# Which split weights of the output projection are kept for the second chunk, and where a PSUM pair's x updates stand

## The chip, the cores and the metric

The kernel runs on one core of a Trainium2 chip. The metric is the device time of one execution in microseconds, lower is better; a version's time is the median of its runs. Five engines work side by side, each through its own instructions in order: TensorE (PE, with its weight loads as PEld), VectorE (DVE), ScalarE (ACT), GpSimd (POOL) and SyncE (SP), which here issues the DMA transfers. PE runs at one of two clocks, 1.2 and 2.4 GHz; the profile gives the granted clock as a share of the higher one.

## The reference

Two layers of a transformer-like trunk, for 128 prompt tokens and 512 latent tokens with the same weights, D_MODEL = 1024. Of a layer, cut to the part around the change:

```python
ga, gb, gc = jnp.split(jax.nn.sigmoid(h @ p['w_gate'] + p['b_gate']), 3, axis=-1)
merged = ga * (oa @ p['w_br_a']) + gb * (ob @ p['w_br_b']) + gc * (oc @ p['w_br_c'])
x = x + g1 * (merged @ p['w_out'])
h2 = _rmsnorm(x, p['norm2']) * (1 + sc2) + sh2
a, g = jnp.split(_dwconv3(h2 @ p['w_up'], p['conv_w'], p['conv_b']), 2, axis=-1)
x = x + g2 * ((jax.nn.silu(a) * g) @ p['w_down'])
```

`oa`, `ob` and `oc` are the outputs of a differential attention, a grouped-query attention and a pooling mixer; `h` is the modulated RMS norm of `x`; `g1`, `g2`, `sc2`, `sh2` are modulations. Everything is in float32.

## The kernel before

All 640 tokens lie side by side in the free dimension, features on the 128 partitions; a matrix of 1024 features is eight tiles of 128 (`ND` = 8). A float32 product is made of three matmuls: `split` (L94 to L96) takes an operand apart into a high part, which ACT copies in the narrower format `F32R`, and a low part, which DVE gets by subtraction; `mm3` (L111 to L114) adds high by low (L112), low by high (L113) and high by high (L114). `load_w` (L98) fetches one tile of weights into a buffer `st` (three of them go round) and splits it into `wh` and `wl`. These normally lie in a ring of five buffers, `wp`, which all weights of the program share; with `keep` they lie in another pool. Matmuls over tokens work on two chunks of 320 (`CH_B`). A `Wide` PSUM tile has two halves of 512 columns, of which 320 are used; three such tiles are used in turn for gates (`gp`), branches (`bp`), the output projection (`wo`) and the MLP (`up`).

A layer runs through these phases: attention, merge, `merged`, `out_phase`, MLP. In the merge each branch is eight tiles: a gate, a branch product, their product on DVE (L812, into the gate's tile `gt`) and, for the last branch, its sum with what the others gave, also on DVE (L813, into one of eight tiles `m32`, in the rows `m`). `merged` splits `m32` into `mh` and `ml`, the low halves of the first chunk on DVE, of the second on POOL.

`out_phase` (L842) then multiplies by w_out: for each chunk eight output tiles, two to a PSUM tile (`wo`), each of 8 x 3 = 24 matmuls. In the first chunk each w_out tile is fetched and split; tiles 0 to 6 are kept for the second chunk in the pool `wk`, and tile 7, which comes first there, is still in the ring. `wk` is opened after the merge's pool `mg` is closed, in the place that `mg` had: seven pairs of weight tiles overlap its buffers for gates, for the split branch outputs and for `m32`, so a split into them waits for the last reader of what lies there. Behind each tile DVE updates x (L862), ACT squares it (L165), and the squares are added (L168 to L171). At a chunk's end `rstd320` makes the norm factor, with two small uses of PE (`stat`, L829, and `bc`, L838 and L839), and `modulate` makes `h2h` and `h2l` (L206 to L209). The first three tiles of w_up follow, whose matmuls for the first chunk run while the second chunk is normalised.

No order is written out by hand: the program is written phase by phase, and a scheduler sets the order of the instructions on each engine from what depends on what. For PSUM the dependence is by whole tile: a matmul that writes half of a `wo` tile comes behind an x update that reads the other half, if the update stands ahead of it in the program. The engines then run in the order so found.

Of the kernel before, what the change touches and what calls it, by code (L numbers as in the profile page):

```python
# [46 lines left out]
def _segs(a, b):  # L47
    out = []
    if a < NP:
        out.append((a, min(b, NP), 0))  # L50
    if b > NP:
        out.append((max(a, NP), b, 1))
    return out
# [3 lines left out]
def trunk_kernel(ctx: ExitStack, tc: tile.TileContext, a: dict):  # L57
# [4 lines left out]
    def tp(name, bufs=1, stack=None, **kw):  # L62
        return (stack or ctx).enter_context(
            tc.tile_pool(name=name, bufs=bufs, reuse_waits="tile", **kw))
# [29 lines left out]
    def split(x, hi, lo, eng=vec):  # L94
        act.activation(hi, x, AF.Copy)  # L95
        eng.tensor_tensor(out=lo, in0=x, in1=hi.bitcast(F32), op=ALU.subtract)  # L96

    def load_w(src, cols, eng=vec, after=None, keep=None):  # L98
        st = wp.tile([P, 1024], F32, tag="st", name="st", bufs=3)
        if after is not None:  # L100
            pool.tensor_copy(st[:, 0:1], after)
        dma(st[:, :cols], src)
        hi = (keep or wp).tile([P, 1024], F32R, tag="wh", name="wh")
        lo = (keep or wp).tile([P, 1024], F32R, tag="wl", name="wl")
        split(st[:, :cols], hi[:, :cols], lo[:, :cols], eng)
        return hi, lo
# [4 lines left out]
    def mm3(out, sh, sl, mh, ml, start, stop):  # L111
        pe.matmul(out, sl, mh, start=start, stop=False)  # L112
        pe.matmul(out, sh, ml, start=False, stop=False)  # L113
        pe.matmul(out, sh, mh, start=False, stop=stop)  # L114
# [727 lines left out]
    def out_phase(l, x, rp, mh, ml, hp, wk, ps_d, first):  # L842


        A2 = scale_cols(l, V_N2, 32, "A2")
        B2 = mods[l][:, 24:32, :]
        h2h, h2l, W = [], [], {}
        for c, (a0, b0) in enumerate(CH_B):
            acc = Acc(rp, 320)
            order = (list(range(8)), [7] + list(range(7)))[c]  # L850
            for n0 in range(0, 8, 2):
                ps = ps_d.tile("wo")
                for j in range(2):
                    n = order[n0 + j]
                    if c == 0:
                        W[n] = load_w(a["w_out"][l, n], 1024, keep=wk if n < 7 else None)
                    hi, lo = W[n]
                    for k in range(ND):
                        ks = slice(k * P, (k + 1) * P)
                        mm3(ps[:, j, :320], hi[:, ks], lo[:, ks], mh[c][:, k], ml[c][:, k], k == 0, k == 7)  # L860
                    for s, e, jj in _segs(a0, b0):
                        vec.scalar_tensor_tensor(out=x[:, n, s:e], in0=ps[:, j, s - a0:e - a0],  # L862
                                                 scalar=mods[l][:, 16 + n, jj:jj + 1], in1=x[:, n, s:e],
                                                 op0=ALU.mult, op1=ALU.add)
                    acc.add(x[:, n, a0:b0], n0 + j == 7)
            h2h.append(hp.tile([P, 8, 320], F32R, tag=f"h{c}", name=f"h2h{c}"))
            h2l.append(hp.tile([P, 8, 320], F32R, tag=f"l{c}", name=f"h2l{c}"))
            modulate(rp, x, rstd320(wk, acc.acc), A2, B2, a0, b0, h2h[c], h2l[c])
        ups = ((0, 0), (1, 0), (0, 1))
        ws = []  # L870
        for c in range(2):
            for i, (part, f) in enumerate(ups):
                if c == 0:
                    ws.append(load_w(a["w_up"][l, part * F_T + f], 1024))
                    first[part, f] = ps_d.tile("up")
                hi, lo = ws[i]
                for k in range(ND):
                    ks = slice(k * P, (k + 1) * P)
                    mm3(first[part, f][:, c, :320], hi[:, ks], lo[:, ks], h2h[c][:, k], h2l[c][:, k], k == 0, k == 7)
        return h2h, h2l  # L880

    def mlp_up(l, f, h2h, h2l, mp, ps_d, first):
        vs = []
# [40 lines left out]
    rp = tp("rp", 2, xst)  # L924
    x = xp.tile([P, ND, T], F32, name="x")
    hst = ExitStack()
    hp = tp("h1p", 1, hst, side="right")
# [3 lines left out]
    ps_d = open_dense(dst)  # L931
# [76 lines left out]
    for l in range(L):  # L1008
        dst.close()
        xst.close()  # L1010
        attention_phase(l, hh, hl, w0)
        w0 = None
        xst = ExitStack()
        xp = tp("xp", 1, xst)
        rp = tp("rp", 2, xst)
        modp = tp("modp", 1, xst)
        x = xp.tile([P, ND, T], F32, name="x")
        dst = ExitStack()
        ps_d = open_dense(dst)
        with ExitStack() as ms:  # L1020
            mp = tp("mg", 1, ms)
            cs = modp.tile([P, 2, 1024], F32, tag="cs", name="cs", bufs=1)
            msteps = mod_steps(l, range(2, 6), modp, cs)
            m32 = merge_phase(l, x, cs, hh, hl, mp, ps_d, msteps)
            hst.close()
            hst = ExitStack()
            hp = tp("h2p", 1, hst, side="right")
            mh, ml = merged(m32, hp)
        first = {}
        with ExitStack() as ms:  # L1030
            h2h, h2l = out_phase(l, x, rp, mh, ml, hp, tp("wk", 7, ms), ps_d, first)
        with ExitStack() as ms:
            mp = tp("mlp", 1, ms)
            ups = {}
            if l + 1 < L:
                msteps = chain(msteps, mod_steps(l + 1, range(2), modp, cs))

            def up_to(f):
                for i in range(len(ups), f):
                    ups[i] = mlp_up(l, i, h2h, h2l, mp, ps_d, first)  # L1040
                    for _ in range(1 if i < GROUPS[0][1] + 2 else 2):
                        next(msteps, None)

            for gi, (f0, f1) in enumerate(GROUPS):
                up_to(min(F_T, f1 + 2))
                fs = [ups[f] for f in range(f0, f1)]
                nf = f1 - f0
                last = gi == len(GROUPS) - 1
                if not last:
                    for n in range(8):  # L1050
                        hi, lo = load_w(a["w_down"][l, n, :, f0 * P:f1 * P], nf * P)
                        ps = ps_d.tile("dn")
                        for c, (a0, b0) in enumerate(CH_B):
                            for i in range(nf):
                                ks = slice(i * P, (i + 1) * P)
                                mm3(ps[:, c, :320], hi[:, ks], lo[:, ks], fs[i][0][:, a0:b0], fs[i][1][:, a0:b0],
                                    i == 0, i == nf - 1)
                        for c, (a0, b0) in enumerate(CH_B):
                            down_add(l, x, n, ps[:, c], a0, b0)
                    continue  # L1060
                hst.close()
                if l + 1 < L:
                    hst = ExitStack()
                    hp = tp("h1p", 1, hst, side="right")
                    hh = hp.tile([P, ND, T], F32R, name="hh")
                    hl = hp.tile([P, ND, T], F32R, name="hl")
                    A1 = scale_cols(l + 1, V_N1, 8, "A1")
                for c, (a0, b0) in enumerate(CH_A):
                    acc = Acc(rp, b0 - a0)
                    for n0 in range(0, 8, 2):  # L1070
                        ps = ps_d.tile("dl")
                        for j in range(2):
                            n = n0 + j
                            hi, lo = load_w(a["w_down"][l, n, :, f0 * P:f1 * P], nf * P)
                            for i in range(nf):
                                ks = slice(i * P, (i + 1) * P)
                                mm3(ps[:, j, :b0 - a0], hi[:, ks], lo[:, ks], fs[i][0][:, a0:b0],
                                    fs[i][1][:, a0:b0], i == 0, i == nf - 1)
                            down_add(l, x, n, ps[:, j], a0, b0)
                            if l + 1 < L:  # L1080
                                acc.add(x[:, n, a0:b0], n == 7)
                                dma(x_dram[:, n, a0:b0], x[:, n, a0:b0])
                            else:
                                dma(a["y"][:, n, a0:b0], x[:, n, a0:b0])
                    if l + 1 < L:
                        rms1_chunk(l + 1, c, rp, x, hh, hl, ps_d, acc, A1)
# [114 lines left out]
```

## Time and profile before

| what | us |
|---|---|
| median of 3 runs | 2310.14 (2308.59 to 2310.95) |
| profiled execution, its own time | 2315.32 |
| its span, from the first to the last instruction | 2312.3 |
| PE busy in the span | 2222.7 |
| mean granted clock of PE | 0.987 |

The stage that the change touches takes, in each layer, about 80 us: from 637.7 to 717.8 us in layer 0 and from 1771 to 1852 us in layer 1, from the last `bp` matmul to the first `up` matmul of the second chunk. Of the profile the waits (who waited for whom), the timeline (each instruction with its start, its duration and the idle time ahead of it) and the windows (busy times and granted clock of a stretch) are used. A matmul's duration overlaps that of the next one; what counts for PE is the step from start to start.

### The profile page before, as it was taken

How to read it: one execution, taken by the hardware profiler on the slowest of the kernel's cores; microseconds unless marked ns; L12 is line 12 of the kernel's file. 1: busy time of each engine (PE TensorE's matmuls, PEld its weight loads, DVE VectorE, ACT ScalarE, POOL GpSimd, SP SyncE). 2: the span in 40 equal slices, each digit the busy share in tenths (PEclk: the TensorE clock that was granted, in tenths of full speed). 3: DMA queues.
4: the chain of work that ended last, by engine and by line, in shares of the span. 5: the costliest groups of instructions: out<-in, count | busy, mean ns of one | idle time of the engine just before them, and what ended most of it. 6: DMA issues, size and time to landing. Idle time of an engine off the chain costs nothing. (4 is left out here: it accounts for less than half of the span.)

```text
span 2312.3 us, 37780 instructions
## 1 busy us (share of the span) xinstructions
PE 2222.7 (96%) x14770; PEld 2165.9 (94%) x14770; DVE 1537.7 (66%) x2885; ACT 962.7 (42%) x1712; POOL 519.4 (22%) x647
## 2 busy tenths in 40 slices
PE   8998999999989999999989989999998999999999
PEld 4898989999989999999979989899998999999999
DVE  6877687569566756765587866864894476554555
ACT  5455555432244423333455546643223354242422
POOL 4652443024021000000047533320421200000000
PEclk8999999999999999999999999999999999999999
DMA  7211223366231233432242112224852132322123
GB/s 262 73 56 59 82 71 105 119 245 221 83 119 58 102 107 121 135 104 86 81 122 83 64 42 83 98 87 151 282 193 77 61 109 92 92 65 91 50 84 114
DMA packets 100469, 250.10 MB, mean 108 GB/s; under 512 B 19266, under 2 KB 32322, under 8 KB 100291
## 3 DMA queue, kind: packets, MB, share of 16 engines
q1 hardware_dynamic: 100292, 247.70, 32.8%
q8 instruction: 116, 1.90, 0.3%
q14 instruction: 61, 0.50, 0.1%
HBM read 224.72 MB, written 22.95 MB: 107 GB/s over the span
## 5 line engine op out<-in xcount | busy, mean ns | idle before, releaser
L112 PE MATMUL up<-h2h,wl 128*128 128x320 f32 x1408 | 432.7, 308 | 3.9 <-ACT h2h L208 2.5
L113 PE MATMUL up<-h2l,wh 128*128 128x320 f32 x1408 | 433.6, 308 | 0.2
L114 PE MATMUL up<-h2h,wh 128*128 128x320 f32 x1408 | 433.6, 308 | 0.0
L95 ACT ACTIVATE wh<-st 128x1024 fp32r<-128x1024 f32 (+3 forms) x320 | 297.6, 937 | 273.9 <-PE dn L114 169.6
L96 DVE TENSOR_TENSOR wl<-st,wh 128x1024 fp32r<-128x1024 f32 (+3 forms) x320 | 356.1, 1117 | 53.8 <-ACT wh L95 53.3
L112 PEld LDWEIGHTS up<-h2h,wl 128*128 128x128 f32 x1408 | 263.5, 188 | 4.6 <-ACT h2h L208 2.7
L113 PEld LDWEIGHTS up<-h2l,wh 128*128 128x128 f32 x1408 | 264.0, 188 | 0.7 <-DVE h2l L209 0.7
L114 PEld LDWEIGHTS up<-h2h,wh 128*128 128x128 f32 x1408 | 264.0, 188 | 0.0
L143 DVE SCALAR_TENSOR_TENSOR junk<-stm,cs 128x1024 bf16<-128x1024 f32 x172 | 221.7, 1289 | 63.0 <-DMA stm<-in_w_mod 60.0
L901 DVE SCALAR_TENSOR_TENSOR v<-u,vecs,v 128x127 f32<-128x127 f32 (+1 forms) x176 | 89.0, 547 | 183.2 <-ACT v L898 183.2
L112 PE MATMUL mm<-wh,hl 128*128 128x384 f32 x480 | 171.5, 357 | 12.4 <-ACT raw L361 8.5
L113 PE MATMUL dn<-al,wh 128*128 128x320 f32 x544 | 168.1, 309 | 0.0
L114 PE MATMUL dn<-ah,wh 128*128 128x320 f32 x544 | 168.1, 309 | 0.0
L112 PE MATMUL dn<-ah,wl 128*128 128x320 f32 x544 | 168.1, 309 | 0.0
L113 PE MATMUL mm<-wl,hh 128*128 128x384 f32 x480 | 165.6, 345 | 2.1 <-DVE wl L96 2.1
L114 PE MATMUL mm<-wh,hh 128*128 128x384 f32 x480 | 165.3, 344 | 0.0
L114 PE MATMUL gp<-hh,wh 128*128 128x320 f32 x480 | 148.5, 309 | 0.0
L112 PE MATMUL gp<-hh,wl 128*128 128x320 f32 x480 | 148.4, 309 | 0.0
L113 PE MATMUL gp<-hl,wh 128*128 128x320 f32 x480 | 148.2, 309 | 0.0
L112 PE MATMUL mmu<-hh,wl 128*128 128x384 f32 (+1 forms) x416 | 133.8, 322 | 3.9 <-ACT up L677 2.0
L114 PE MATMUL mmu<-hh,wh 128*128 128x384 f32 (+1 forms) x416 | 130.9, 315 | 0.0
L113 PE MATMUL mmu<-hl,wh 128*128 128x384 f32 (+1 forms) x416 | 130.1, 313 | 0.0
(232 smaller groups left out, 5434.9 us busy)
## 6 DMA issues: line engine op xcount, KB each, us to landing
stm<-in_w_mod SPq DMA_DIRECT2D x88, 512.0 KB, 4.3
st<-in_w_up SPq DMA_DIRECT2D x88, 512.0 KB, 3.6
st<-in_w_gate SPq DMA_DIRECT2D x48, 512.0 KB, 3.8
st<-in_w_unit SPq DMA_DIRECT2D x48, 384.0 KB, 3.2
st<-in_w_down SPq DMA_DIRECT2D x48, 320.0 KB, 2.9
st<-in_w_br SPq DMA_DIRECT2D x24, 512.0 KB, 3.6
st<-in_w_down SPq DMA_DIRECT2D x32, 384.0 KB, 3.2
st<-in_w_out SPq DMA_DIRECT2D x16, 512.0 KB, 4.3
```

Of the source, the lines that this page charges most:

```text
L95: act.activation(hi, x, AF.Copy)
L96: eng.tensor_tensor(out=lo, in0=x, in1=hi.bitcast(F32), op=ALU.subtract)
L112: pe.matmul(out, sl, mh, start=start, stop=False)
L113: pe.matmul(out, sh, ml, start=False, stop=False)
L114: pe.matmul(out, sh, mh, start=False, stop=stop)
L143: vec.scalar_tensor_tensor(out=junk, in0=st, scalar=1.0, in1=cs[:, j], op0=ALU.mult, op1=ALU.mult, accum_out=col)
L901: vec.scalar_tensor_tensor(out=v[:, s + 1:e], in0=u[:, s:e - 1], scalar=cw[0], in1=v[:, s + 1:e], op0=ALU.mult, op1=ALU.add)
```

## The change

`wk` holds four pairs of weight tiles instead of seven, for tiles 2 to 5. Tiles 0, 1, 6 and 7 go into the ring. The second chunk goes through the tiles in the order 6, 7, 2, 3, 4, 5, 0, 1; tiles 6 and 7 are then still in the ring, and tiles 0 and 1 are fetched and split a second time. By the addresses of the built programs, `wk` before reached over the gates' tiles, the branch operands and into `m32`; now it ends ahead of `m32`, but still lies over the others. The x updates of a PSUM pair stand in a loop of their own behind the matmuls of both tiles. The first w_up tiles have moved into a function of their own with the same code.

```diff
@@ out_phase @@
-            order = (list(range(8)), [7] + list(range(7)))[c]
+            order = (list(range(8)), (6, 7, 2, 3, 4, 5, 0, 1))[c]
             for n0 in range(0, 8, 2):
                 ps = ps_d.tile("wo")
                 for j in range(2):
                     n = order[n0 + j]
-                    if c == 0:
-                        W[n] = load_w(a["w_out"][l, n], 1024, keep=wk if n < 7 else None)
+                    if c == 0 or n < 2:
+                        W[n] = load_w(a["w_out"][l, n], 1024, keep=wk if 2 <= n < 6 else None)
                     hi, lo = W[n]
                     for k in range(ND):
                         ks = slice(k * P, (k + 1) * P)
                         mm3(ps[:, j, :320], hi[:, ks], lo[:, ks], mh[c][:, k], ml[c][:, k], k == 0, k == 7)
+                for j in range(2):
+                    n = order[n0 + j]
                     for s, e, jj in _segs(a0, b0):
                         vec.scalar_tensor_tensor(out=x[:, n, s:e], in0=ps[:, j, s - a0:e - a0],
...
+        if first is not None:
+            up_first(l, h2h, h2l, ps_d, first)
+        return h2h, h2l
+
+    def up_first(l, h2h, h2l, ps_d, first):
+
         ups = ((0, 0), (1, 0), (0, 1))
...
-            h2h, h2l = out_phase(l, x, rp, mh, ml, hp, tp("wk", 7, ms), ps_d, first)
+            h2h, h2l = out_phase(l, x, rp, mh, ml, hp, tp("wk", 4, ms), ps_d, first)
```

The scheduler's order changes in three places that matter here. Rows give the line, the instruction, what it writes and reads, and how often it stands there in a row.

DVE in layer 0, the last branch of the merge (two of its eight tiles), before:

```order
L96 TENSOR_TENSOR wl<-st,wh 128x1024
L812 TENSOR_TENSOR gt<-bp,gt 128x640
L813 TENSOR_TENSOR m_5599<-m_5599,gt 128x640
L812 TENSOR_TENSOR gt<-bp,gt 128x640
L813 TENSOR_TENSOR m_5569<-m_5569,gt 128x640
```

and after:

```order
L96 TENSOR_TENSOR wl<-st,wh 128x1024 x2
L812 TENSOR_TENSOR gt<-bp,gt 128x640
L813 TENSOR_TENSOR m_5599<-m_5599,gt 128x640
L96 TENSOR_TENSOR wl<-st,wh 128x1024
L812 TENSOR_TENSOR gt<-bp,gt 128x640
L813 TENSOR_TENSOR m_5569<-m_5569,gt 128x640
```

The two added splits are those of w_out's tiles 0 and 1; on ACT the copies that belong to them have moved likewise, between the sigmoids of the last gates.

DVE some ten instructions later, where the merge ends and the output projection begins, before:

```order
L812 TENSOR_TENSOR gt<-bp,gt 128x640
L813 TENSOR_TENSOR m_5506<-m_5506,gt 128x640
L96 TENSOR_TENSOR ml_7154<-m_5506,mh_7152 128x320
L96 TENSOR_TENSOR wl<-st,wh 128x1024 x5
L862 SCALAR_TENSOR_TENSOR x<-wo,mod_88,x 128x128
L862 SCALAR_TENSOR_TENSOR x<-wo,mod_88,x 128x192
```

and after:

```order
L812 TENSOR_TENSOR gt<-bp,gt 128x640
L813 TENSOR_TENSOR m_5506<-m_5506,gt 128x640
L96 TENSOR_TENSOR ml_7154<-m_5506,mh_7152 128x320
L96 TENSOR_TENSOR wl<-st,wh 128x1024 x3
L864 SCALAR_TENSOR_TENSOR x<-wo,mod_88,x 128x128
L864 SCALAR_TENSOR_TENSOR x<-wo,mod_88,x 128x192
L864 SCALAR_TENSOR_TENSOR x<-wo,mod_88,x 128x128
L864 SCALAR_TENSOR_TENSOR x<-wo,mod_88,x 128x192
```

Five splits stood behind the merge's last split, those of tiles 0 to 4; now there are three, of tiles 2 to 4, and the x updates of two tiles stand together.

PE in layer 0's output projection, first chunk, at the start of tile 1 (the numbers tell buffers apart; `wl_7198` and `wl_7234`, after it `wl_7228`, are tiles 0 and 1, `wl_7270` is tile 2, and `wo_7194` is the PSUM tile of tiles 0 and 1), before:

```order
L114 MATMUL wo_7266<-mh0_7152,wh_7269 128x320
L112 MATMUL wo_7337<-mh0_7152,wl_7341 128x320
L113 MATMUL wo_7337<-ml0_7154,wh_7340 128x320
L112 MATMUL wo_7194<-mh0_7152,wl_7234 128x320
L113 MATMUL wo_7194<-ml0_7154,wh_7233 128x320
```

and after:

```order
L113 MATMUL wo_7194<-ml0_7154,wh_7197 128x320
L114 MATMUL wo_7194<-mh0_7152,wh_7197 128x320
L112 MATMUL wo_7194<-mh0_7152,wl_7228 128x320
L113 MATMUL wo_7194<-ml0_7154,wh_7227 128x320
L114 MATMUL wo_7194<-mh0_7152,wh_7227 128x320
```

Before, tile 1 came behind tile 2 and the first two matmuls of tile 4; now the tiles of a pair follow each other, and the pairs stand in the order of the program. Layer 1 has the same order in all these places.

PE in layer 1's attention, ahead of a block of the input projection (`mmu`; `tr` are transposes, `sc` scores, `pv` products with values), before:

```order
L545 MATMUL sc<-qk 128x128 x8
L113 MATMUL pv<-pl,v_12949 128x128
L114 MATMUL pv<-ph,v_12949 128x128
L292 MATMUL tr<-ident,dup 128x128
L112 MATMUL mmu<-hh,wl 128x256
```

and after:

```order
L545 MATMUL sc<-qk 128x128 x8
L113 MATMUL pv<-pl,v_12961 128x128
L114 MATMUL pv<-ph,v_12961 128x128
L292 MATMUL tr<-ident,dup 128x128 x5
L112 MATMUL mmu<-hh,wl 128x256
```

Four transposes of the next group have moved ahead of the block; further places near it move with them on PE, ACT and DVE. Layer 0's attention has the order that it had.

## Rows read from the trace of the kernel before

**Rows 1.** Page: engines busy, share, instructions; a DMA group, KB each, us to land.

```profile
PE 2222.7 (96%) x14770; PEld 2165.9 (94%) x14770; DVE 1537.7 (66%) x2885; ACT 962.7 (42%) x1712; POOL 519.4 (22%) x647
...
st<-in_w_out SPq DMA_DIRECT2D x16, 512.0 KB, 4.3
```

**Rows 2.** Waits, 600 to 730 us, PE: waiter, releaser, us in all, times, longest.

```profile
PE wo L112 <- DVE wl L96: 6.1, 1, 6.1
PE up L112 <- ACT h2h L208: 1.2, 1, 1.2
PE wo L112 <- DVE x L862: 0.9, 1, 0.9
```

**Rows 3.** Timeline, PE, layer 0: start, duration, instruction, idle time before, releaser.

```profile
637.09 0.31 PE L114 MATMUL bp<-oh,wh 128*128 128x320 f32 x1
...
637.53 0.31 PE L114 MATMUL bp<-oh,wh 128*128 128x320 f32 x1
643.96 0.60 PE L112 MATMUL wo<-mh,wl 128*128 128x320 f32 x1 [6.13 <-DVE wl L96]
...
647.57 0.47 PE L113 MATMUL wo<-ml,wh 128*128 128x320 f32 x1
647.83 0.35 PE L114 MATMUL wo<-mh,wh 128*128 128x320 f32 x1
```

**Rows 4.** Windows: length, busy PE, PEld, DVE, ACT, POOL; PEclk; DMA, GB/s.

```profile
640.00:660.00 20.00, 16.04 (x97) 16.07 (x98) 12.79 (x16) 10.52 (x12) 2.73 (x3) 0.83 0.59 188
1334.00:1344.20 10.20, 8.61 (x39) 8.23 (x40) 8.03 (x17) 3.27 (x10) 0.17 (x4) 0.50 0.17 51
```

**Rows 5.** Timeline, PE, layer 1: the same place as rows 3.

```profile
1770.92 0.31 PE L114 MATMUL bp<-oh,wh 128*128 128x320 f32 x1
1777.36 0.61 PE L112 MATMUL wo<-mh,wl 128*128 128x320 f32 x1 [6.13 <-DVE wl L96]
...
1781.20 0.31 PE L114 MATMUL wo<-mh,wh 128*128 128x320 f32 x1
```

**Rows 6.** Timeline, DVE, then ACT, layer 0, from the merge's end on.

```profile
638.73 1.40 DVE L813 TENSOR_TENSOR m<-m,gt 128x640 f32<-128x640 f32 x1
640.67 0.53 DVE L96 TENSOR_TENSOR ml<-m,mh 128x320 fp32r<-128x320 f32 x1 [0.54 <-ACT mh L95]
641.97 4.12 DVE L96 TENSOR_TENSOR wl<-st,wh 128x1024 fp32r<-128x1024 f32 x3 [0.78 <-ACT wh L95]
...
654.75 1.23 DVE L96 TENSOR_TENSOR wl<-st,wh 128x1024 fp32r<-128x1024 f32 x1 [0.99 <-ACT wh L95]
640.16 0.83 ACT L95 ACTIVATE mh<-m 128x320 fp32r<-128x320 f32 x2 [2.47 <-DVE m L813]
640.90 2.93 ACT L95 ACTIVATE wh<-st 128x1024 fp32r<-128x1024 f32 x3
648.13 1.06 ACT L95 ACTIVATE wh<-st 128x1024 fp32r<-128x1024 f32 x1 [4.29 <-DMA st<-in_w_out]
```

**Rows 7.** Timeline, SP's queue, layer 0: issue and time until the group's last landing.

```profile
643.84 8.32 SPq L102 DMA_DIRECT2D st<-in_w_out  x5
```

**Rows 8.** Timeline, DVE, layer 0, in the merge's last branch.

```profile
623.86 0.82 DVE L812 TENSOR_TENSOR gt<-bp,gt 128x640 f32<-128x640 f32 x1 [8.95 <-PE bp L114]
```

**Rows 9.** Timeline, PE, the waits in the first chunk of layers 0 and 1.

```profile
668.12 0.42 PE L112 MATMUL wo<-mh,wl 128*128 128x320 f32 x1 [0.87 <-DVE x L862]
1802.12 0.41 PE L112 MATMUL wo<-mh,wl 128*128 128x320 f32 x1 [1.54 <-DVE x L862]
```

**Rows 10.** Timeline, DVE, layer 0, end of the second chunk.

```profile
708.33 0.55 DVE L862 SCALAR_TENSOR_TENSOR x<-wo,mod,x 128x320 f32<-128x320 f32 x1 [6.49 <-PE wo L114]
...
713.58 0.16 DVE L832 TENSOR_SCALAR ms<-stat 128x3 f32<-128x3 f32 x1 [3.54 <-PE stat L829]
```

**Rows 11.** Waits, 1320 to 1420 us, PE: the first and last of eight.

```profile
PE pt L495 <- DVE qk L296: 2.8, 1, 2.8
...
PE pt L467 <- DVE qk L300: 0.3, 1, 0.3
```

More of the change, by code (lines that the diff above doesn't have):

```diff
@@ L879, in out_phase @@
                     mm3(first[part, f][:, c, :320], hi[:, ks], lo[:, ks], h2h[c][:, k], h2l[c][:, k], k == 0, k == 7)
-        return h2h, h2l
     def mlp_up(l, f, h2h, h2l, mp, ps_d, first):
```

## The prediction

> **What bounds the kernel now.** The page comes first: TensorE (PE) is busy for 96% of the span, and the next engine for 66% [rows 1]. So a microsecond is to be had only where PE stands still or runs slowly, and work moved to the other engines is free as long as PE isn't made to wait for it. The question is therefore where PE waits inside the stage that the diff touches, the output projection. The waits from 600 to 730 us give PE's longest three there [rows 2]: one of 6.1 us for a split weight (`wl`) ahead of the first `wo` matmul, one of 0.9 us for an x update, one of 1.2 us for `h2h`. The diff can reach all three.
>
> The timeline shows the first of them in full [rows 3]. The last `bp` matmul starts at 637.53, the first `wo` at 643.96, and fourteen matmuls later, at 647.83, the step is back at the 0.147 us that it had before (637.09 to 637.53 are three); ahead of that it is 0.26 us (647.57 to 647.83). The stretch from 640 to 660 us has a mean granted clock of 0.83 [rows 4]: between its two levels, 1.2 and 2.4 GHz, so 20 x 0.17 / 0.5 = 6.8 us of it ran at the lower one. Since the long steps end at 647.83, the clock fell at about 641, when PE had stood idle for some 3 us. The whole delay is 647.83 - 637.68 (where the next matmul would have started) - 14 x 0.147 = 8.09 us, of which 6.28 us are idle and 1.81 us slow matmuls. Layer 1 repeats it: 1770.92, 1777.36, 1781.20, by the same sum 8.07 us [rows 5].
>
> Why PE waited is read from the other engines [rows 6]. VectorE (DVE) multiplies the last branch tile by its gate, behind the last `bp` matmul, and adds it (638.73), ScalarE (ACT) makes the high halves of the merged sum (640.16), DVE the low half (640.67 to 641.20). Only behind that stand the first splits of w_out: ACT from 640.90, DVE from 641.97, three in 4.12 us. The data of three of them had long landed, since the next load of w_out was issued only at 643.84 [rows 7]. So the operand of the projection was ready at 641.20, its weight 2.7 us later.
>
> **The change part by part.** *Weights clear of the merge.* The pool of split weights in the place of the merge's buffers has four tiles instead of seven, and tiles 0 and 1 now lie in the ring that all weights use. In the new order their splits stand among the merge's last products, where DVE is idle for 8.95 us ahead of one of them, waiting for PE [rows 8]: 2 x 1.23 us fit there. The first `wo` matmul then waits for no split. It may start at 637.68; each of the eight products of a tile needs one merged tile, and only the last needs the one made at 641.20. Seven products are 21 matmuls, 3.09 us, so PE comes to the last product at 640.77. Its first matmul needs the high half, made by about 640.6; the second comes at 640.92 and needs the low half at 641.2 plus some 0.06 us of passing on: 0.35 us of waiting is left. What is late next is thus the merge chain itself, which isn't shortened. After so short a wait I take the clock to stay up: it fell in the two waits of 6.13 us, where the first matmul behind took 0.60 us [rows 3], while behind those of 0.87 and 1.54 us it took 0.42 and 0.41 [rows 9]. Gain: 8.09 - 0.35 = 7.74 and 8.07 - 0.35 = 7.72, together 15.46 us.
>
> *Do the following weights come in time?* Tiles 2 to 4 are landed and are split from 640.99 on, in ACT's and DVE's present pace (4.12 us for three), so about 643.4, 644.7 and 646.1. PE needs them after two, three and four tiles of 24 x 0.147 = 3.53 us: 645.1, 648.6, 652.2. Tile 5 is the first whose load must be issued then: buffer free at about 643.4, 4.3 us to land [rows 1], 1.06 us on ACT and 1.23 us on DVE [rows 6] make 650, needed at 655.7. From there three buffers go round in 4.3 + 1.06 + 1.23 = 6.6 us, 2.2 us a tile against 3.53. The smallest cover is the 1.7 us at tile 2.
>
> *Two more loads a layer.* Tiles 0 and 1 are fetched and split again: 2 x 512 KB on SP's queue, 2 x 1.06 us of ACT, 2 x 1.23 us of DVE. Five such loads were done in 8.32 us [rows 7], so the two take some 3.3 us of a queue that has 28.2 us (a whole chunk of eight tiles) until they are needed. The w_up loads behind them on SP are due after the chunk, and wait for ring buffers freed by its first tiles. Nil; if all of it came through to PE it would be 2 x 3.3 = 6.6 us.
>
> *x of a pair behind both tiles.* An x update reads a PSUM tile that the second tile of the pair writes, so before the change the second had to wait for the first's x; the scheduler put other tiles between, and where they ran out there are the waits at 668.12 and 1802.12. They are 0.87 and 1.54 us, and the matmul behind each takes 0.42 and 0.41 us instead of 0.31 [rows 3]: 0.87 + 0.11 + 1.54 + 0.10 = 2.62 us [rows 9]. Now a pair's tiles run back to back, and the next pair writes another of three PSUM tiles. A pair's updates take twice 0.55 us on DVE [rows 10], and the PSUM tile is wanted again after two more pairs, 14 us. Gain: the 2.62 us.
>
> The last pair of a chunk now has two x updates behind the last matmul instead of one: 0.55 us on DVE and about 0.5 us for the second square. Before, the statistic came from the x update at 708.33 to 713.58, where DVE waited 3.54 us for PE to come to it [rows 10]. It now stands behind 41 matmuls of w_up, 6.0 us, instead of 32, and the broadcast behind 31 more. So there is cover, and the 1.2 us for `h2h` [rows 2], which the broadcast at the end of the cover sets, stays in both layers.
>
> *What the scheduler moved elsewhere.* Layer 0's attention is as before, but in layer 1's the order differs around 1320 to 1420 us: four transposes of the next group are pulled ahead of a projection block. In that stretch PE waits 2.8 us for a `qk` sum, and down to 0.3 us for seven other things [rows 11], and from 1334.0 to 1344.2 the granted clock is 0.50 [rows 4]. The moved transposes need a DVE sum that now is issued earlier; I can't say from the order whether the stretch gains or loses. Bounds: with the clock back it would gain half of 10.2 us, 5.1 us; with its eight waits, 7.8 us in all, doubled it would lose 7.8 us. I take 0, since the same instructions run on the same operands.
>
> **The sum.** 15.46 + 2.62 = 18.1 us. The profiled execution is 2315.32 us (span 2312.3 and 3.0 around it), so 2297.2 there; it lies 5.2 us above the median of the runs, 2310.14, and the wanted time is the median: 2310.14 - 18.1 = **2292.0 us**.
>
> **The rivals.** *The clock falls all the same.* For it: the change puts a stop at every start of `wo`, however short, and the clock did fall here. Against it: the waits of 0.87 and 1.54 us were not followed by slow matmuls. If it fell for as long as before, 6.8 us (of which 14 long steps are 3.7 us, while the rest lay in the idle time and cost nothing), PE, now working through all of it, would lose half, 3.4 us a layer: 18.1 - 6.8 = 11.3 us are left, 2298.8 us. The Trainium skill ("TensorE: Matmul & The Clock Gate", section "A second HAM failure mode: psum-queue depth-cycling") speaks against this change: it says of another kernel that short idle moments between groups of matmuls, with PSUM tiles cycled, were enough to make the clock swing between its levels. The pairs here cycle three PSUM tiles. This case's trace so far speaks against the rule at such waits [rows 9]; by it the time would be this rival's.
>
> *The change doesn't do what it says.* The splits of tiles 0 and 1 stand early in the order, but each needs a ring buffer that an earlier branch weight frees, and the merge chain might set the start in a way that the order doesn't show. Then only the 2.62 us are won: 2307.5. Against it: the ring's next buffers hold weights whose matmuls ended at least one branch tile earlier, and DVE's idle time ahead of one shows that it takes over 8.95 us with its gate [rows 8].
>
> *The supply of weights becomes the bound.* Two more loads a layer come through: 18.1 - 6.6 = 11.5 us, 2298.6. Against it stand 2.2 us of supply against 3.53 of use.
>
> *Slower.* The one place that could do it is layer 1's attention, where instructions of four engines stand in a new order and each engine runs in order. The price: 18.1 us to undo and 4.6 us more (0.2%, about what a measurement of this kernel can tell from no change), so it decides from 22.7 us of new stalls on. That is three times the 7.8 us that PE now waits there. If each of the eight waits grew by the 2.8 us of the largest, 22.4 us would be lost: just short of it, 2314.4.
>
> **How the numbers follow.** Forecast, with layer 1's attention between -5.1 and +7.8: 0.70. The clock falls: 0.12. Weight supply: 0.06. No effect at the start: 0.07. Attention takes it all or more: 0.05, of which 0.04 slower. The first three are faster by over 0.2% (below 2305.5), and a small part of the last but one, with some gain in the attention: 0.90. Within 0.2%: 0.06. Slower: 0.04. The range goes from 2286 (2292.0 - 5.1, and the two waits of 0.35 us gone) to 2302, which takes in the two rivals near 2298.7 with half of the attention's loss.
>
> **What would show it.** Right: no wait of PE for `wl` at the start of `wo`, one under 0.6 us for `ml` in its place; steps of 0.147 us from there on; no wait of `wo` for x; w_out loads twenty in all; `up` still waiting 1.2 us for `h2h`. Wrong: a granted clock of 0.5 in the first `wo` matmuls (the first rival), a wait for `wl` at tile 2 or at tiles 0 and 1 of the second chunk (supply), PE's waits from 1320 to 1420 us far from 7 us (the scheduler).

## The result, and the profile after

| | before | after |
|---|---|---|
| median of the runs, us | 2310.55 (2308.59 to 2312.27, 4 runs) | 2292.81 (2291.01 to 2294.58, 4 runs) |
| span of the profiled execution, us | 2312.3 | 2292.5 |
| PE busy, us | 2222.7 | 2219.7 |
| loads of w_out | 16 | 20 |

The ratio is 0.9923, with a 95% interval from 0.9906 to 0.9941: 17.7 us less, where 18.1 us were forecast (2292.0 us).

The waits of PE from 600 to 730 us answer to [rows 2]. The columns are the waiting engine and line, the releaser, microseconds in all, times, longest:

```profile
PE up L112 <- ACT h2h L208: 1.2, 1, 1.2
PE up L112 <- ACT v L905: 0.7, 1, 0.7
PE wo L113 <- DVE ml L96: 0.2, 1, 0.2
```

The wait for a split weight is gone, and so is the wait for x. A wait for `ml`, the low half of the merged sum, stands in their place. The 0.7 us for `v` stood there before as well (L898, fourth in the list). Layer 1's list is the same. The timeline of PE at the start of `wo` in layer 0 answers to [rows 3] (start, duration, instruction, idle time before it):

```profile
636.11 0.31 PE L114 MATMUL bp<-oh,wh 128*128 128x320 f32 x1
636.26 0.31 PE L112 MATMUL wo<-mh,wl 128*128 128x320 f32 x1
...
639.19 0.31 PE L114 MATMUL wo<-mh,wh 128*128 128x320 f32 x1
639.34 0.39 PE L112 MATMUL wo<-mh,wl 128*128 128x320 f32 x1
639.90 0.42 PE L113 MATMUL wo<-ml,wh 128*128 128x320 f32 x1 [0.17 <-DVE ml L96]
640.15 0.31 PE L114 MATMUL wo<-mh,wh 128*128 128x320 f32 x1
```

The first `wo` follows the last `bp` after 0.15 us. Seven products run through, the eighth product's second matmul comes 0.56 us after its first and the next 0.25 us after that, so 0.41 + 0.10 = 0.51 us are left of the 8.09. Layer 1 reads 0.55 and 0.26 at the same place. The profile shows only 0.17 us as idle, because it counts from the modelled end of the matmul before (0.39 us after its start), and the next would have started 0.147 us after that start. In the same way the 0.87 us of [rows 9] stand for a step that was longer by 1.03.

Where the splits went is seen on DVE in the merge (of [rows 8], the idle time before the products):

```profile
610.12 1.23 DVE L96 TENSOR_TENSOR wl<-st,wh 128x1024 fp32r<-128x1024 f32 x1 [6.05 <-ACT wh L95]
611.82 0.82 DVE L812 TENSOR_TENSOR gt<-bp,gt 128x640 f32<-128x640 f32 x1 [0.47 <-PE bp L114]
...
620.68 1.23 DVE L96 TENSOR_TENSOR wl<-st,wh 128x1024 fp32r<-128x1024 f32 x1 [7.18 <-ACT wh L95]
622.38 0.83 DVE L812 TENSOR_TENSOR gt<-bp,gt 128x640 f32<-128x640 f32 x1 [0.47 <-PE bp L114]
```

Tiles 0 and 1 are ready at 611.35 and 621.91, 25 and 18 us ahead of their use. The products behind them still wait for PE (0.47 us), so the splits delayed nothing.

The gain can be had in one number by measuring the same stage in both traces, from the last `bp` matmul to the first `up` matmul of the second chunk, which is the same work on both sides. The windows (stretch, its length, busy times of PE, PEld, DVE, ACT and POOL, granted clock, DMA share, GB/s) for both layers, of the kernel before:

```profile
637.50:717.84 80.34, 72.11 (x480) 71.36 (x478) 42.86 (x84) 28.16 (x50) 18.84 (x20) 0.96 0.27 86
1770.90:1851.83 80.93, 72.03 (x480) 71.29 (x478) 42.54 (x84) 27.97 (x50) 19.64 (x20) 0.96 0.27 85
```

and of the changed kernel:

```profile
636.10:707.65 71.55, 70.15 (x480) 69.60 (x478) 42.59 (x84) 27.97 (x50) 18.98 (x20) 1.00 0.31 96
1760.40:1831.95 71.55, 70.16 (x479) 69.61 (x477) 43.75 (x84) 27.83 (x50) 18.99 (x20) 1.00 0.30 97
```

The stage is 8.79 and 9.38 us shorter, 18.2 us together, the clock is at the higher level throughout, and both layers now take the same time. The profiled spans differ by 19.8 us; the 1.6 us that are missing lie outside the stage (see the last section).

### The profile page after: what moved, and what is told of

It reads as the page before. It is cut to its first block, busy times and chain, and to the rows that moved or that the text cites. A ratio compares the mean times of both kernels' runs of the same rounds, so it can differ in the third digit from the quotient of the medians.

```text
span 2292.5 us, 37818 instructions
## 1 busy us (share of the span) xinstructions
PE 2219.7 (97%) x14770; PEld 2162.9 (94%) x14770; DVE 1548.0 (68%) x2889; ACT 966.1 (42%) x1716; POOL 515.5 (22%) x647
## 5 line engine op out<-in xcount | busy, mean ns | idle before, releaser
L96 DVE TENSOR_TENSOR wl<-st,wh 128x1024 fp32r<-128x1024 f32 (+3 forms) x324 | 361.5, 1120 | 85.0 <-ACT wh L95 84.3
```

## The experiments

Of each run the same stage was measured as above, beside the median.

**The weights' part alone.** Four pairs kept and the new order of tiles, but x behind each tile. Against the changed kernel:

```diff
-                for j in range(2):
-                    n = order[n0 + j]
                     for s, e, jj in _segs(a0, b0):
```

> The weights' part alone: four pairs in wk, order 6, 7, 2, 3, 4, 5, 0, 1, but x behind each tile as before. Theory (start of wo 15.46 us, x waits 2.62 us, the two independent): no wait for wl at the start, and 15.46 us of the gain stay: 2310.5 - 15.5 = 2295 us. In this order tile 1 follows tile 0 at once in the same PSUM tile, so waits of wo for x of about 1 us a layer should be in the trace, as in the kernel before. Rival (the pair's x is what frees the start, because it is what lets the tiles run in order): a wait for wl of several us stays, 2305 us or more.

Measured: 2296.78 us (2295.76 to 2297.65), ratio to the kernel before 0.9934, interval 0.9917 to 0.9952. The timeline of PE in layer 0, a little after the start of `wo`:

```profile
638.40 0.41 PE L113 MATMUL wo<-ml,wh 128*128 128x320 f32 x1 [0.17 <-DVE ml L96]
638.65 0.31 PE L114 MATMUL wo<-mh,wh 128*128 128x320 f32 x1
639.73 0.41 PE L112 MATMUL wo<-mh,wl 128*128 128x320 f32 x1 [0.77 <-DVE x L862]
```

and the stage in layer 0 (72.59 us in layer 1):

```profile
634.60:707.18 72.58, 70.40 (x479) 69.60 (x477) 43.57 (x84) 27.71 (x50) 19.30 (x20) 1.00 0.31 95
```

No wait for `wl` is left in either layer: the weights' part frees the start by itself. The wait for x has moved to where tile 1 follows tile 0, and costs a step of 1.08 instead of 0.15 us, in both layers. The stage is 16.1 us shorter than before: the whole start, and 0.9 us of x waits a layer where there were 1.0 and 1.7. The rival falls. By the median this run is 4.0 us behind the changed kernel, by the stage 2.1; for what may be the rest see layer 1's attention in the next section.

**The x part alone.** x behind both tiles of a pair, seven pairs kept and the old order. Against the kernel before:

```diff
+                for j in range(2):
+                    n = order[n0 + j]
                     for s, e, jj in _segs(a0, b0):
```

> The x part alone: x behind both tiles of a pair, seven pairs in wk and the old order of tiles. Theory: the wait of 6.1 us for wl and the half clock behind it stay in both layers, the waits of wo for x are gone: 2310.5 - 2.6 = 2307.9 us. Rival (x part carries the start too): below 2300 us.

Measured: 2306.67 us (2305.14 to 2308.73), ratio 0.9981, interval 0.9972 to 0.9990. PE's waits from 600 to 730 us:

```profile
PE wo L112 <- DVE wl L96: 6.1, 1, 6.1
PE up L112 <- ACT h2h L208: 1.0, 1, 1.0
PE up L112 <- ACT v L905: 0.7, 1, 0.7
```

The stage in both layers:

```profile
635.20:715.12 79.92, 72.76 (x480) 72.19 (x478) 43.57 (x84) 28.36 (x50) 18.29 (x20) 0.96 0.27 86
1767.20:1846.13 78.93, 71.78 (x480) 71.21 (x478) 43.27 (x84) 28.36 (x50) 18.27 (x20) 0.96 0.28 87
```

The wait for x is gone, the wait for the weight is what it was. The stage is 2.4 us shorter, 0.4 in layer 0 and 2.0 in layer 1; in layer 0 the slow matmuls happened to last for 21 steps instead of 14. The median gives 4.2 us (against 2310.86, 15 runs of the kernel before) with an interval from 2.3 to 6.5 us, which holds the 2.6 expected. The two parts add up: 2.4 and 16.1 us make 18.5, together they gave 18.2.

**Which place has to be clear, and what the second loads cost.** Tiles 0 and 1 stay in the ring for both chunks, tiles 2 to 7 are kept in six pairs that reach over the merged sum again, nothing is loaded twice. Against the changed kernel:

```diff
-            order = (list(range(8)), (6, 7, 2, 3, 4, 5, 0, 1))[c]
+            order = (list(range(8)), (0, 1, 2, 3, 4, 5, 6, 7))[c]
...
-                    if c == 0 or n < 2:
-                        W[n] = load_w(a["w_out"][l, n], 1024, keep=wk if 2 <= n < 6 else None)
+                    if c == 0:
+                        W[n] = load_w(a["w_out"][l, n], 1024, keep=wk if n >= 2 else None)
...
-            h2h, h2l = out_phase(l, x, rp, mh, ml, hp, tp("wk", 4, ms), ps_d, first)
+            h2h, h2l = out_phase(l, x, rp, mh, ml, hp, tp("wk", 6, ms), ps_d, first)
```

> Tiles 0 and 1 stay in the ring for both chunks, tiles 2 to 7 are kept in wk (six pairs, which reach into the place of the merged sum again), order 0 to 7 in both chunks, no second load. Theory (what counts is that the two tiles used first lie outside the merge's place; being clear of the merged sum does not count, and the second loads are hidden): 2292.8 us, within 2 us, no wait for wl. Rival 1 (clear of the merged sum is what counts): a wait for wl of 1 to 6 us a layer, 2295 to 2305 us. Rival 2 (the second loads cost something): up to 6.6 us less than after, 2286 us.

Measured: 2293.48 us (2288.83 to 2297.14), ratio 0.9920, interval 0.9900 to 0.9940, not to be told from the changed kernel by its time, with runs up to 8 us apart. PE's waits of the same stretch:

```profile
PE up L112 <- ACT h2h L208: 1.0, 1, 1.0
PE up L112 <- ACT v L905: 0.7, 1, 0.7
PE wo L113 <- DVE ml L96: 0.2, 1, 0.2
```

So it doesn't matter whether the kept weights lie over the merged sum. What counts is that the two tiles used first lie outside the merge's place. And the two further loads a layer are hidden in the stage: without them it is 0.1 us a layer shorter (71.4 us in both), most of it in the wait for `h2h`, 1.0 us instead of 1.2, as in the run before this one, which has no second loads either.

**One tile clear instead of two.** Five pairs kept (tiles 1 to 5), only tile 0 loaded again:

```diff
-            order = (list(range(8)), (6, 7, 2, 3, 4, 5, 0, 1))[c]
+            order = (list(range(8)), (6, 7, 1, 2, 3, 4, 5, 0))[c]
...
-                    if c == 0 or n < 2:
-                        W[n] = load_w(a["w_out"][l, n], 1024, keep=wk if 2 <= n < 6 else None)
+                    if c == 0 or n < 1:
+                        W[n] = load_w(a["w_out"][l, n], 1024, keep=wk if 1 <= n < 6 else None)
...
-            h2h, h2l = out_phase(l, x, rp, mh, ml, hp, tp("wk", 4, ms), ps_d, first)
+            h2h, h2l = out_phase(l, x, rp, mh, ml, hp, tp("wk", 5, ms), ps_d, first)
```

> Only tile 0 clear of the merge's place: five pairs in wk (tiles 1 to 5), order 6, 7, 1, 2, 3, 4, 5, 0 in the second chunk, only tile 0 loaded again. Theory: PE runs through tile 0 while the merge ends, about 24 x 0.147 + 0.4 = 3.9 us, and then waits for tile 1's split, which can't start before the merge's last split: about 1.9 us a layer, with the clock staying up: 2292.8 + 3.8 = 2296.6 us. Rival 1 (one tile is cover enough): 2292.8 us. Rival 2 (the clock falls behind such a wait): 3.4 us more a layer, 2303 us.

Measured: 2301.68 us (2298.43 to 2306.53), ratio 0.9957, interval 0.9943 to 0.9972. The timeline of PE, layer 0:

```profile
639.57 0.31 PE L114 MATMUL wo<-mh,wh 128*128 128x320 f32 x1
641.95 0.64 PE L112 MATMUL wo<-mh,wl 128*128 128x320 f32 x1 [2.07 <-DVE wl L96]
642.38 0.47 PE L113 MATMUL wo<-ml,wh 128*128 128x320 f32 x1
...
644.78 0.45 PE L113 MATMUL wo<-ml,wh 128*128 128x320 f32 x1
645.05 0.32 PE L114 MATMUL wo<-mh,wh 128*128 128x320 f32 x1
```

The wait came as expected, 2.07 us for tile 1's split. But the clock fell behind it: one step of 0.43 and ten of 0.27 us from 641.95 on. Layer 1 shows it too, with a difference: there four matmuls after the wait ran at full speed first.

```profile
1770.71 0.42 PE L112 MATMUL wo<-mh,wl 128*128 128x320 f32 x1 [2.07 <-DVE wl L96]
1770.96 0.31 PE L113 MATMUL wo<-ml,wh 128*128 128x320 f32 x1
1771.11 0.31 PE L114 MATMUL wo<-mh,wh 128*128 128x320 f32 x1
1771.26 0.31 PE L112 MATMUL wo<-mh,wl 128*128 128x320 f32 x1
1771.41 0.41 PE L113 MATMUL wo<-ml,wh 128*128 128x320 f32 x1
1771.61 0.47 PE L114 MATMUL wo<-mh,wh 128*128 128x320 f32 x1
```

The stage is 3.7 and 3.9 us longer than in the changed kernel, of which 2.2 are the idle step and about 1.5 the slow matmuls. That is less than the 3.4 us a layer of the second rival, which had the whole 6.8 us of [rows 4] in mind, but its mechanism is the one that happened. My theory of this run fell in that point.

**How long a wait the clock stands.** Somewhere between the 0.5 us that the changed kernel loses here and the 2.1 us of this run the first rival of the prediction would have come true. Copies of the last merged tile onto itself, put on DVE ahead of its split, move the end of the merge. Against the changed kernel (one, two and five copies):

```diff
+        for _ in range(1):
+            vec.tensor_copy(m32[7], m32[7])
         for c, (a0, b0) in enumerate(CH_B):
             for n in range(8):
```

> The changed kernel with one copy of the last merged tile onto itself put on VectorE ahead of its split, so that the merge's end comes later and the wait in front of the eighth product of tile 0 (0.42 us in the changed kernel) grows by a copy of 128x640, some 0.6 to 0.8 us: about 1.1 us a layer. Theory (the clock stays up behind short waits and falls behind longer ones; it stayed up behind 0.4 us and fell behind 2.1 us in the run with one tile clear): no slow matmuls, the stage longer by the copy alone. Rival (any wait ahead of wo costs the clock): steps of 0.27 us for some microseconds.

> As the run with one copy, with two: a wait of about 1.7 us a layer. It lies between the 1.54 us of the kernel before, behind which the clock stayed up, and the 2.1 us of the run with one tile clear, behind which it fell. Theory: undecided by the runs so far, either no slow matmuls or about 3.4 us of them (1.7 us lost); the rival expects slow matmuls here and with one copy.

> As the run with one copy, with five: a wait of about 3.7 us a layer. Theory: the clock falls, a wait of 3.7 us costs 1.7 to 3.4 us more in slow matmuls, 5 to 7 us a layer. Rival (the time lost is the wait alone): 3.3 us a layer more than the changed kernel.

These are single executions, read in the trace and not by their times (2295.54, 2302.25 and 2305.93 us). PE's longest wait at the start of `wo`, the same in both layers, with one, two and five copies:

```profile
PE wo L112 <- ACT mh L95: 0.9, 1, 0.9
```

```profile
PE wo L112 <- ACT mh L95: 2.0, 1, 2.0
```

```profile
PE wo L112 <- ACT mh L95: 3.5, 1, 3.5
```

and the windows around the start of `wo` in layer 0, in the same order:

```profile
636.00:660.00 24.00, 22.95 (x155) 22.46 (x155) 16.63 (x25) 12.43 (x17) 7.61 (x8) 1.00 0.65 187
```

```profile
636.00:660.00 24.00, 22.05 (x138) 21.50 (x138) 17.76 (x25) 12.41 (x17) 6.88 (x7) 0.93 0.57 183
```

```profile
638.00:650.00 12.00, 8.35 (x45) 7.85 (x44) 9.07 (x15) 5.05 (x8) 2.81 (x3) 0.86 0.33 92
```

With one copy the clock stays at 1.00, and the time lost against 0.147 us a step is 1.5 us a layer, the copy (1.05 us) and the 0.5 us from before it. So not every stop at this place costs the clock. With two copies the clock falls in both layers, 24 x 0.07 / 0.5 = 3.4 us of it at the lower level; the wait was 2.0 us, not the 1.7 that I had expected, since a copy took 1.05 us. With five it falls for 12 x 0.14 / 0.5 = 3.4 us as well. Of a wait of 3.5 us and a fall of the clock, 5.7 and 5.4 us a layer are lost in all: a longer wait costs itself, and the slow matmuls 1.4 to 1.7 us more, in each of the six falls behind waits of 2.0 to 3.5 us at this place. They aren't a fixed price: behind the 6.1 us of the kernel before, where the low clock lasted for 6.8 us, part of it in the wait, they cost 1.8 us, and 2.7 in layer 0 of the run with the x part alone.

## Why the prediction was right, point by point

- **What bounds the kernel.** PE's waits in the stage; 18.2 us of them and of slow matmuls were taken out, and 17.7 us came through in the median. Nothing else became the bound.
- **The start of `wo`.** 8.09 and 8.07 us with 0.35 us left in each were forecast. Over the first 130 matmuls the changed kernel loses 0.48 and 0.47 us against 0.147 us a step, the kernel before 8.10 and 8.04. The left-over wait is for `ml`, at the eighth product, as worked out. It is 0.13 us longer than forecast (0.16 by its two steps, 0.51): 0.10 us are the longer step behind the wait, which the sum had counted for the x waits and not here, and the low half was ready 3.74 us after the start of the last `bp` matmul, where 3.67 us had been read before. The 0.06 us of passing on stood in the sum without a row; 0.05 us were measured (639.85 to 639.90).
- **The clock stays up.** It did, 1.00 in the whole stage. The reason given was too weak, though. I had taken the 0.42 us of the first matmul behind the waits of 0.87 and 1.54 us as a sign that the clock had not fallen. The run with one tile clear shows a first matmul of 0.42 us and three full ones more behind a wait of 2.07 us, and the slow steps only after them. What holds is the granted clock of the stretch behind those waits, in the windows of the kernel before:

```profile
660.00:690.00 30.00, 29.13 (x200) 28.81 (x199) 15.42 (x36) 10.45 (x20) 9.10 (x9) 1.00 0.33 104
1795.00:1825.00 30.00, 28.46 (x196) 28.14 (x195) 15.25 (x38) 9.85 (x21) 9.89 (x9) 1.00 0.30 92
```

- **The weights come in time.** No wait for `wl` from the first `wo` matmul to the last in either layer, with tile 2 having the smallest cover. It was 1.3 us in layer 0 and not 1.7, since the first split behind the merge took 1.90 us (640.60 to 642.50, used from 643.82), more than a third of the 4.12 us for three. The run with one tile clear shows how it looks without cover.
- **The second loads.** Forecast at nil; the run without them gave the same time, and a stage shorter by 0.1 us a layer.
- **x of a pair.** 2.62 us were forecast. What the stage gave beyond the start is 18.2 - 15.2 = 3.0 us. Measured as steps, 1.18 and 0.26 us in layer 0 and 1.85 and 0.25 us in layer 1 had stood where 0.147 now stands four times, which makes 2.95 us and is all of it. The sum had taken the idle time as the profile shows it, which begins only at the end of the matmul before, and so missed 0.16 us of each wait.
- **The end of the stage.** The wait for `h2h` is 1.2 us in both layers, as forecast. On DVE the statistic still waited for PE:

```profile
701.20 0.16 DVE L832 TENSOR_SCALAR ms<-stat 128x3 f32<-128x3 f32 x1 [3.00 <-PE stat L829]
702.33 0.56 DVE L835 TENSOR_TENSOR dg<-ident,rr 128x384 f32<-128x384 f32 x1 [0.97 <-POOL rr L118]
706.45 1.46 DVE L206 SCALAR_TENSOR_TENSOR ht<-x,A,bc 128x320 f32<-128x320 f32 x3 [3.57 <-PE bc L839]
```

  The factor `dg` was ready at 702.89 and the broadcast was issued only at 705.65, where the order had put it. The wait for `h2h` may be shortened there; it was not tried.
- **Layer 1's attention.** Taken at nil between -5.1 and +7.8. It gained 1.85 us: the same 1200 matmuls, in the kernel before (first line) and in the changed one (second), where the stretch at the lower clock (third) became shorter, 20 x 0.17 / 0.5 = 6.8 us instead of 10.2:

```profile
1216.80:1408.60 191.80, 182.26 (x1202) 176.33 (x1200) 139.19 (x307) 97.14 (x228) 98.41 (x131) 0.97 0.22 71
1208.40:1398.40 190.00, 181.65 (x1202) 175.84 (x1201) 139.21 (x305) 96.97 (x229) 95.46 (x130) 0.98 0.23 72
1324.00:1344.00 20.00, 16.85 (x102) 15.87 (x102) 16.07 (x34) 8.58 (x25) 2.76 (x6) 0.83 0.14 46
```

  The run with six pairs kept has the changed kernel's order of matmuls there and took 189.6 us. The five runs whose order is that of the kernel before, but for at most 10 of the 1200, took 191.2 to 192.0 us, the weights' part alone among them, and the one with one copy, which has a third order, 189.9 us. So the order that the scheduler found is worth about 2 us, by one profile each. What cancelled it is a place that neither the order shown ahead of the prediction nor its sum has: at the start of layer 1, ahead of this stretch, 6 of 200 matmuls stand in another order too. They took 48.3 us before (from 1168.5 us) and 50.1 us after (from 1158.3 us), with one wait of 5.3 us for `raw` (L361) where the longest had been 2.0. The run with the x part alone, with the old order there, took 47.3 us, the others 48.6 to 50.8. From the stage's end in layer 0 to the first `bp` of layer 1 the changed kernel thus took only 0.4 us less. That nil came out right is luck: two things moved by almost 2 us each, in opposite directions.
- **The rivals.** The first was nearer than its 0.12 says. Its mechanism is real at this very place: at a wait of 2 us the clock falls. The change leaves 0.5 us, and one tile less in the ring would have left 2.1. The rival's price was too high, though: a fall costs about 1.5 us a layer here and not 3.4, which would have left 15 us of the gain. The prediction set 1.54 against 6.13 us, though the kernel before has waits between them. The wait of 2.8 us of [rows 11] reaches into the low stretch from 1334.0 us on of [rows 4]:

```profile
1335.58 0.48 PE L495 MATMUL pt<-ident,w 128*128 128x128 f32 x1 [2.80 <-DVE qk L296]
```

  The same wait stands in layer 0, up to 200.41 us, and one of 2.02 us up to 1210.94 us, with a granted clock of 0.50 behind each (200.8 to 207.6, 1211.2 to 1214.5 us). By these the clock was at risk from about 2 us on, four times what the change leaves. The other rivals did not come.

The Trainium skill ("TensorE: Matmul & The Clock Gate", "A second HAM failure mode: psum-queue depth-cycling") says of another kernel that short idle moments between groups of matmuls made the clock swing. At the pairs of `wo` no run here shows it: in the changed kernel the stage has a clock of 1.00 with three PSUM tiles in turn, and with one copy two stops of 0.9 and 0.15 us change nothing. What comes nearest in this case is the merge of layer 0, in the last section.

## What to carry to other kernels

Where a new pool is opened in the place of one just closed, its first tiles wait for the last reader of the old one; the tiles used first belong elsewhere, as many as cover the end of the old phase (here two, 7 us of matmuls, against 6.4 us from the last `bp` until the first kept weight was split; one left a wait of 2 us), and the rest may lie where they like. To judge whether a wait costs the clock as well, look at the granted clock of the microseconds behind it, not at the first matmul. To check a sum that is made of waits, measure one stage between the same two instructions in both traces: the stage gave 18.2 us where spans, which carry the spread of everything else, gave 19.8. And where a scheduler sets the order, compare the other stretches too: here two of them moved by almost 2 us each and hid one another.

## What the runs showed of the hardware

Ahead of `wo` matmuls, the clock stayed at 1.00 behind waits of 0.2, 0.8, 0.9 and 1.5 us; behind waits of 2.0, 2.1, 3.5 and 6.1 us it fell, each time in both layers. The rest of the nine traces, from 90 us on, agrees: 37 waits of PE are 1.95 us or longer, and with all of them the clock was at the lower level in the wait or within 2 us behind it. Below that the edge isn't sharp. A wait of 1.8 us in the attention stands twice in each trace. Behind 17 of the 18 the clock stayed, and behind one, in layer 0 of the changed kernel, it fell (0.50 from 316.0 to 319.3 us):

```profile
314.50 0.30 PE L467 MATMUL pt<-ident,w 128*128 128x128 f32 x1 [1.83 <-DVE pl L456]
```

The clock doesn't have to fall during the wait: in layer 1 with one tile clear, and with five copies in layer 0, PE had resumed and run some matmuls at full speed before the slow ones came. With five copies the windows before and from there on read

```profile
641.00:644.00 3.00, 1.46 (x8) 1.23 (x9) 1.61 (x4) 2.10 (x4) 0.87 (x1) 1.00 0.00 0
644.00:647.50 3.50, 3.50 (x16) 3.50 (x15) 3.21 (x3) 1.58 (x2) 0.00 (x0) 0.53 0.41 109
```

so the half speed fell wholly on work, although PE had waited for 3.5 us up to 642.43.

The 1.6 us by which the spans differ more than the stage are what is left of differences in both directions, in part of this kind. From 495 to 520 us, in layer 0's merge, which the change doesn't touch, the granted clock was 0.93 in the kernel before, 1.00 in the changed one:

```profile
495.00:520.00 25.00, 23.23 (x144) 22.71 (x145) 24.54 (x34) 7.00 (x8) 11.84 (x12) 0.93 0.87 330
```

```profile
495.00:520.00 25.00, 23.21 (x155) 22.61 (x155) 24.54 (x34) 7.13 (x9) 11.84 (x11) 1.00 0.88 328
```

That is 25 x 0.07 / 0.5 = 3.5 us at the lower level, 1.75 us of time. It shows again (0.93) in the run with six pairs kept, and in layer 0 of none of the other runs. In the kernel before it stands behind three waits of PE for branch operands, 0.3 to 0.8 us each; the changed kernel has three such waits as well, of 0.3 to 1.0 us, and kept its clock. In the other direction, the 500 matmuls around the fall at 316 us took the changed kernel 83.5 us, the other eight 82.0 to 82.2. So such falls vary from execution to execution, and one profile against another carries a microsecond or two that no change has made. What decides it was not tried.
